# A two-layer hybrid mixer on one core: accumulators that share a PSUM tile are evacuated together

## The chip, the cores and the metric

The kernel runs on one core of a Trainium2 chip. The metric is the device time of one execution in microseconds: the median of three runs was 1438.51 us, the lowest 1437.9, the highest 1441.57.

## The reference, cut to what matters

Two layers (`DEPTH = 2`) work on 512 latent tokens ("x") and 256 context tokens ("c"), each 1024 channels wide. All arithmetic is float32. Each layer normalises both streams, projects them with one wide matrix `w_in`, runs three branches (a convolution of width 31, a chunked linear attention called GLA, and grouped-query attention), merges them with sigmoid gates and multiplies by `w_out`:

```python
hx = rms_norm(xs, norm_g) * (1 + scale_x[:, None]) + shift_x[:, None]
px = split_cols(hx @ w_in + b_in)
...
xs = xs + gate_x[:, None] * merge(px, ya_x, yb_x, yc_x)
if need_ctx:
    cs = cs + gate_c * merge(pc, ya_c, yb_c, yc_c)
```

`merge` ends with `@ w_out`. In the second layer the context stream is not written back, and attention queries are needed for the latent stream alone. The result is the latent stream.

## The kernel before

**Precision.** Every float32 operand of a large product is split into a rounded part and a remainder (`hi` and `lo`, `whi` and `wlo`), and a product is the sum of three: `hi*whi`, `lo*whi`, `hi*wlo`. A step of 256 input channels (two blocks of 128) for a tile of 128 tokens and 512 output columns is thus six matmuls (`tm_terms`, L566): four on `whi`, two on `wlo`.

**Weights.** `g_load` brings one unit of weights after the other into two `raw` buffers, `g_split` casts it into `whi` (ScalarE or VectorE) and subtracts for `wlo` (VectorE). There are three buffers of each.

**Two kinds of projections.** Most jobs compute channel-major results through single-bank PSUM tiles (`pg`, two of them; `pm`, two more). The jobs of class `Wide` (L650) compute token-major results: `QJob` (queries, with a bias added on the way out) and `OutJob` (the product with `w_out`). A `Wide` job holds one accumulator of 128 tokens by 512 columns for each token tile, and goes through the input channels in four rounds, one weight unit each; in a round every token tile gets its six matmuls in turn.

**Where the accumulators lie.** `banks` (L656) takes PSUM for them. The tag `p2` has two buffers of 1024 columns, and each of them holds the accumulators of two token tiles, side by side (`b[:, 0]` and `b[:, 1]`); `pg` and `pm` hold one each. `done` gives a `p2` buffer back when both of its accumulators have been read. The trace calls tiles of the tag `p2` just `p`. These jobs have pairs in `p2`:

- `QJob` of the first layer: six token tiles, two pairs in `p2` and two in `pg`
- `QJob` of the second layer: four token tiles, two pairs
- `OutJob` of the first layer for x: block 0 (columns 0 to 511) in two pairs, block 1 in `pg` and `pm`
- `OutJob` of the first layer for c: blocks 0 and 1, one pair each
- `OutJob` of the second layer for x: block 0 in two pairs, block 1 in `pg` and `pm`; the kernel ends with it

**Evacuation.** In the last round (`q == 3`), `mm` (L678) starts a thread `evac` for a token tile as soon as its matmuls have been written into the program. For a `QJob` it adds the bias on VectorE and writes to SBUF. For an `OutJob` (`out_ev`, L1868) VectorE multiplies the accumulator by the gate `gb` into `tg`, adds the result to the residual, and SyncE stores it. `gb` is a broadcast made on TensorE in the fourth round (`gate`, L1936) and copied out of PSUM by ScalarE or VectorE (`gev`).

**What sets the order.** The program is written at build time by a planner, `Weaver`: threads (Python generators) of different priorities announce the engine that they want next, and the planner, with its own table of costs, resumes whichever can run first. The order in which threads issue is the order of each engine's queue on the chip. `gemm` (L541) gives way to other threads after every three matmuls. Where a step may go to ScalarE or VectorE ("E"), the planner takes the one that it thinks is free first. The sequence of the large jobs is a list (`P["o0"]`, `P["o1"]`). The waits between the engines are set by the framework from the tiles that each instruction reads and writes; they are not written in the kernel.

**After the first layer's output jobs.** The c output jobs run on TensorE while the x stream is normalised for the second layer (`norm_g`, `norm_t`: squares on ScalarE and VectorE, a reciprocal root on GpSimd, scaling, transposes on TensorE, then the split into `hx`). The context follows the same way once its last output block is there, into `hc`. The second layer starts with `c2 m7 q1 q0`: two channel-major jobs that need `hx`, the `QJob`, and the key/value job, which needs `hc` too.

Of the kernel before, what the change touches and what calls it, by code (L numbers as in the profile page):

```python
# [105 lines left out]
class Weaver:  # L106
# [22 lines left out]
    def spawn(self, gen, prio):  # L129
        ready = self.cur.fin + self.LAT if self.cur else self.now  # L130
        th = _Thread(gen, prio, ready)
        i = 0
        while i < len(self.threads) and self.threads[i].prio <= prio:
            i += 1
        self.threads.insert(i, th)
        self._resume(th, keep=True)
# [35 lines left out]
    def need(self, *tags):  # L172
        def ok():
            return all(sum(a <= self.now for a in self.avail[t]) >= n for t, n in tags)
        if not ok():
            yield ok
        for t, n in tags:
            for _ in range(n):
                self.avail[t].remove(min(self.avail[t]))
# [11 lines left out]
    def free(self, tag, n=1, low=False):  # L191
        if low:
            self.low -= n
        t = self.cur.fin + self.LAT
        self.avail[tag] += [t] * n
        self.marks.append(t)
# [5 lines left out]
    def wait(self, *evs):  # L202
        def ok():
            return all(e.t is not None and e.t <= self.now for e in evs)
        if not ok():
            yield ok
# [100 lines left out]
def hybrid_kernel(ctx: ExitStack, tc: tile.TileContext, x, c, ctx_in, c_ctx, norm_g, w_mod, b_mod,  # L307
# [75 lines left out]
    need, free, wait, fire, spawn = W.need, W.free, W.wait, W.fire, W.spawn  # L383
# [157 lines left out]
    def gemm(ps, terms, start=True, stop=True):  # L541
        n = len(terms)
        for i, (l, r) in enumerate(terms):
            if i % 3 == 0:
                yield "+P"
            PE.matmul(ps, lhsT=l, rhs=r, start=start and i == 0, stop=stop and i == n - 1)
# [19 lines left out]
    def tm_terms(w, h, cols, k0):  # L566
        wh, wl = w
        hh, hl = h
        t = []
        for k in range(wh.shape[1]):  # L570
            t += [(hh[:, k0 + k, cols], wh[:, k]), (hl[:, k0 + k, cols], wh[:, k])]
        for k in range(wh.shape[1]):
            t += [(hh[:, k0 + k, cols], wl[:, k])]
        return t
# [75 lines left out]
    class Wide:  # L650
# [5 lines left out]
        def banks(self, n, tags):  # L656

            took, left = [], n
            for t, k in tags:
                m = 2 if t == "p2" else 1  # L660
                while k and left > 0:
                    took.append((t, min(m, left)))
                    left -= m
                    k -= 1
            yield from need(*[(t, sum(x == t for x, _ in took)) for t in dict(took)])
            ps = []
            for t, m in took:
                hold = [m]
                b = {"p2": p2, "pg": pg, "pm": pm}[t]([m, 512])

                def done(hold=hold, t=t):
                    hold[0] -= 1
                    if hold[0] == 0:
                        free(t)
                ps += [(b[:, i], done) for i in range(m)]
            return ps

        def mm(self, tiles, ps, ready, evac, mid=None):  # L678
            for q, (i, u) in enumerate(zip(self.order, self.us)):
                yield from wait(u.ev)  # L680
                if mid is not None and q == 3:
                    yield from mid()
                for t, (h, rows) in enumerate(tiles):
                    yield from ready(i, t)
                    w, hl = u.w, h
                    yield from gemm(ps[t][0], tm_terms(w, hl, rows, 2 * i), start=q == 0, stop=q == 3)
                    if q == 3:
                        spawn(evac(t, *ps[t]), 1)
                free("whi")
                free("wlo")  # L690

# [1385 lines left out]
```

## Time and profile before

| | |
|---|---|
| median of three runs | 1438.51 us |
| the profiled execution | 1437.46 us |
| its span, first to last instruction | 1435.7 us |
| TensorE busy | 1384.6 us (96%) in 9076 matmuls |
| VectorE busy | 1059.7 us (74%) |
| ScalarE busy | 574.3 us (40%) |
| GpSimd busy | 233.8 us (16%) |
| granted TensorE clock | 1.000 |

The profiled execution lies 1.8 us over its span, and 1.05 us below the median. Every arithmetic instruction passes through one recording helper, so all rows carry its line, L302; they are told apart by their tiles. In a row of the timeline, the first number is the start in us, the second the time from the first start to the last end of a run of like instructions, then the engine, and in brackets the idle time of the engine before it and what ended that.

### The profile page before, as it was taken

How to read it: one execution, taken by the hardware profiler on the slowest of the kernel's cores; microseconds unless marked ns; L12 is line 12 of the kernel's file. 1: busy time of each engine (PE TensorE's matmuls, PEld its weight loads, DVE VectorE, ACT ScalarE, POOL GpSimd, SP SyncE). 2: the span in 40 equal slices, each digit the busy share in tenths (PEclk: the TensorE clock that was granted, in tenths of full speed). 3: DMA queues.
4: the chain of work that ended last, by engine and by line, in shares of the span. 5: the costliest groups of instructions: out<-in, count | busy, mean ns of one | idle time of the engine just before them, and what ended most of it. 6: DMA issues, size and time to landing. Idle time of an engine off the chain costs nothing.

```text
span 1435.7 us, 23778 instructions
## 1 busy us (share of the span) xinstructions
PE 1384.6 (96%) x9076; PEld 1187.9 (83%) x9076; DVE 1059.7 (74%) x1863; ACT 574.3 (40%) x1113; POOL 233.8 (16%) x325
## 2 busy tenths in 40 slices
PE   3999999999999999999999999999999999999998
PEld 2789888888998878788888778988888988778886
DVE  4437966689946999963676485877679999997664
ACT  4514455554215324442322163345554155344320
POOL 1004212231000041310031020512221000231200
PEclk9999999999999999999999999999999999999999
DMA  9931233123342335554654365432224344345752
GB/s 271 289 110 51 72 103 90 47 58 89 92 128 75 103 114 165 158 159 154 213 192 146 122 197 181 125 108 79 61 59 115 83 114 136 103 139 193 256 198 73
DMA packets 219157, 187.49 MB, mean 131 GB/s; under 512 B 15400, under 2 KB 181922, under 8 KB 219044
## 3 DMA queue, kind: packets, MB, share of 16 engines
q1 hardware_dynamic: 218748, 185.87, 42.8%
q8 instruction: 71, 1.16, 0.3%
q14 instruction: 42, 0.34, 0.1%
q10 hardware_dynamic: 296, 0.11, 0.0%
HBM read 151.86 MB, written 34.08 MB: 130 GB/s over the span
## 4 chain that ended last, share of the span: by engine, by line
PE 50%; DVE 5%; POOL 1%; issue 1%; ACT 1%; DMA 0%; SPq 0%; DVEq 0%; POOLq 0%
PE pg L302 36%; PE p L302 9%; PE pm L302 4%; DVE r L302 3%; POOL sm L302 1%; DVE tg L302 1%; DVE wlo L302 1%; DVE t L302 0%; DMA r<-oad 0%; DVE zt L302 0%; POOL r L302 0%; ACT r L302 0%; ACT tg L302 0%; DVE sm L302 0%; ACT whi L302 0%
## 5 line engine op out<-in xcount | busy, mean ns | idle before, releaser
L302 PE MATMUL pg<-hx,whi 128*128 128x512 f32 x1504 | 385.8, 397 | 0.3 <-DVE r L302 0.3
L302 PEld LDWEIGHTS pg<-hx,whi 128*128 128x128 f32 x1504 | 272.3, 188 | 54.8 <-issue 2.8
L302 DVE SCALAR_TENSOR_TENSOR r<-r,tp,r 128x768 f32<-128x768 f32 (+29 forms) x240 | 201.2, 883 | 0.2
L302 PE MATMUL pg<-hx,wlo 128*128 128x512 f32 x752 | 196.4, 394 | 0.0
L302 ACT CAST whi<-raw 128x512 fp32r<-128x512 f32 (+1 forms) x195 | 115.0, 619 | 191.6 <-PE pg L302 113.4
L302 DVE TENSOR_TENSOR wlo<-raw,whi 128x1024 fp32r<-128x1024 f32 (+1 forms) x140 | 173.7, 1241 | 17.1 <-ACT whi L302 16.2
L302 PEld LDWEIGHTS pg<-hx,wlo 128*128 128x128 f32 x752 | 138.3, 188 | 27.7 <-issue 0.4
L302 ACT ACTIVATE tg<-pg,hv 128x256 f32<-128x256 f32 (+1 forms) x116 | 71.8, 619 | 186.7 <-PE pg L302 163.5
L302 DVE TENSOR_TENSOR r<-r,r 128x512 f32<-128x512 f32 (+8 forms) x208 | 119.1, 599 | 24.7 <-DMA r<-ogd 9.0
L302 PE MATMUL pg<-r,whi 128*128 128x512 f32 (+1 forms) x576 | 124.8, 358 | 0.3 <-DVE tg L302 0.2
L302 POOL TENSOR_SCALAR r<-r,sm 128x768 f32<-128x768 f32 (+1 forms) x80 | 78.6, 985 | 273.1 <-DVE sm L302 222.5
L302 PEld LDWEIGHTS pg<-r,whi 128*128 128x128 f32 x576 | 96.1, 188 | 17.6 <-DVE tg L302 0.7
L302 PE MATMUL pg<-hc,whi 128*128 128x256 f32 x768 | 105.0, 285 | 0.0
L302 DVE TENSOR_TENSOR r<-p,r 128x384 fp32r<-128x384 f32 (+2 forms) x152 | 77.8, 544 | 33.8 <-ACT r L302 27.6
L302 PEld LDWEIGHTS pg<-hc,whi 128*128 128x128 f32 x768 | 98.4, 190 | 3.3 <-issue 0.4
L302 ACT ACTIVATE r<-p,sm 128x768 f32<-128x768 f32 (+1 forms) x80 | 65.4, 818 | 83.8 <-DVE sm L302 81.1
L302 PE MATMUL p<-r,r 64*64 64x128 f32 (+3 forms) x800 | 84.8, 299 | 4.1 <-DVE r L302 2.9
L302 POOL TENSOR_TENSOR r<-r,r 128x512 f32<-128x512 f32 (+1 forms) x33 | 48.3, 1469 | 224.3 <-DVE r L302 219.4
L302 DVE CAST whi<-raw 128x512 fp32r<-128x512 f32 (+1 forms) x85 | 35.5, 422 | 64.1 <-PE p L302 26.8
L302 PE MATMUL pg<-whi,hx 128*128 128x272 f32 (+2 forms) x480 | 82.4, 309 | 0.0
L302 PE MATMUL pm<-r,r 128*128 128x256 f32 (+3 forms) x832 | 81.4, 279 | 0.2
L302 PEld LDWEIGHTS p<-r,r 64*64 64x64 f32 (+2 forms) x800 | 65.7, 163 | 17.5 <-issue 7.4
(171 smaller groups left out, 2091.6 us busy)
## 6 DMA issues: line engine op xcount, KB each, us to landing
raw<-in_w_in SPq DMA_DIRECT2D x116, 512.0 KB
r<-in_w_mod SPq DMA_DIRECT2D x64, 192.0 KB
thd<-tg SPq DMA_DIRECT2D x48, 256.0 KB
raw<-in_w_out SPq DMA_DIRECT2D x24, 512.0 KB
r<-thd SPq DMA_DIRECT2D x24, 384.0 KB
r<-in_w_mod SPq DMA_DIRECT2D x16, 384.0 KB
sgd<-tg SPq DMA_DIRECT2D x24, 256.0 KB
r<-thd SPq DMA_DIRECT2D x24, 256.0 KB
```

What stands on the lines that cost most here:

```text
L302: return real(*a, **k)
```

## The change

The list that `banks` returns says for each accumulator, beside its PSUM slice and its `done`, whether it is the last one of its PSUM tile. In the last round `mm` no longer starts an accumulator's `evac` thread right behind its own matmuls: it keeps the token tiles in `full`, and starts their threads, in order, once the matmuls of the last accumulator of the same PSUM tile have been written. For tiles in `pg` and `pm`, which hold one accumulator, nothing changes. The list of jobs and the parameters of the planner stay as they are.

```diff
@@ banks
-                ps += [(b[:, i], done) for i in range(m)]
+                ps += [(b[:, i], done, i == m - 1) for i in range(m)]
@@ mm
+                full = []
                 for t, (h, rows) in enumerate(tiles):
                     yield from ready(i, t)
                     w, hl = u.w, h
                     yield from gemm(ps[t][0], tm_terms(w, hl, rows, 2 * i), start=q == 0, stop=q == 3)
-                    if q == 3:
-                        spawn(evac(t, *ps[t]), 1)
+                    full.append(t)
+                    if q == 3 and ps[t][2]:
+                        for t in full:
+                            spawn(evac(t, *ps[t][:2]), 1)
+                        full = []
```

## Rows read from the trace of the kernel before

**Rows 1.** The page: busy time of each engine, with share of span and instructions.
```profile
PE 1384.6 (96%) x9076; PEld 1187.9 (83%) x9076; DVE 1059.7 (74%) x1863; ACT 574.3 (40%) x1113; POOL 233.8 (16%) x325
```

**Rows 2.** The page: the chain that ended last, share of span by engine.
```profile
PE 50%; DVE 5%; POOL 1%; issue 1%; ACT 1%; DMA 0%; SPq 0%; DVEq 0%; POOLq 0%
```

**Rows 3.** Stretches: start:end, length; busy us of PE, PEld, DVE, ACT, POOL; clock.
```profile
520.00:590.00 70.00, 67.20 (x640) 57.64 (x640) 66.67 (x95) 26.00 (x47) 16.54 (x29) 1.00 0.56 158
...
896.00:960.00 64.00, 64.00 (x483) 56.23 (x482) 50.63 (x103) 23.95 (x52) 19.42 (x36) 1.00 0.42 120
...
1090.00:1230.00 140.00, 139.72 (x776) 122.11 (x775) 137.21 (x225) 55.90 (x96) 1.73 (x3) 1.00 0.43 118
1230.00:1300.00 70.00, 65.05 (x610) 51.85 (x609) 64.04 (x119) 28.45 (x47) 20.89 (x33) 1.00 0.39 129
```

**Rows 4.** What PE waited for: us in total, times, longest.
```profile
PE p L302 <- DVE tg L302: 6.9, 6, 2.7
PE p L302 <- DVE r L302: 5.4, 10, 1.0
```

**Rows 5.** Timeline of PE: two gemms of six, first round of block 0.
```profile
780.38 1.07 PE L302 MATMUL p<-whi,hx 128*128 128x512 f32 x4
...
781.74 1.07 PE L302 MATMUL p<-whi,hx 128*128 128x512 f32 x4
```

**Rows 6.** Timeline of PE: last round of that job, the first pair's second gemm.
```profile
798.96 0.86 PE L302 MATMUL p<-whi,hx 128*128 128x512 f32 x3
800.67 0.50 PE L302 MATMUL p<-whi,hx 128*128 128x512 f32 x1 [0.85 <-DVE tg L302]
...
801.47 1.07 PE L302 MATMUL p<-whi,hx 128*128 128x512 f32 x4
```

**Rows 7.** Timeline of DVE beside it.
```profile
799.93 0.69 DVE L302 TENSOR_TENSOR tg<-p,r 128x512 f32<-128x512 f32 x1 [1.60 <-PE p L302]
```

**Rows 8.** Timeline of PE: first and last `QJob` stall, first `OutJob` stall at the end.
```profile
107.97 0.50 PE L302 MATMUL p<-whi,hx 128*128 128x512 f32 x1 [0.78 <-DVE r L302]
...
894.44 0.50 PE L302 MATMUL p<-whi,hx 128*128 128x512 f32 x1 [0.79 <-DVE r L302]
...
1403.66 0.51 PE L302 MATMUL p<-whi,hx 128*128 128x512 f32 x1 [0.85 <-DVE tg L302]
```

**Rows 9.** Timeline of DVE: the first layer's `QJob`, its first pair.
```profile
105.19 1.29 DVE L302 TENSOR_TENSOR r<-p,r 128x512 f32<-128x512 f32 x2 [1.29 <-PE p L302]
```

**Rows 10.** Timeline of PE: block 0 of the c output job.
```profile
838.39 0.86 PE L302 MATMUL p<-whi,hc 128*128 128x512 f32 x3
841.98 0.49 PE L302 MATMUL p<-whi,hc 128*128 128x512 f32 x1 [2.73 <-DVE tg L302]
...
842.77 0.85 PE L302 MATMUL p<-whi,hc 128*128 128x512 f32 x3
843.47 1.03 PE L302 MATMUL pm<-cst,r 128*128 128x128 f32 x8
```

**Rows 11.** Timeline of ACT and DVE beside it.
```profile
840.63 0.57 ACT L302 COPY r<-pm 128x512 f32<-128x512 f32 x1
841.10 0.72 ACT L302 ACTIVATE r<-r,sm 128x512 f32<-128x512 f32 x1
...
841.23 0.69 DVE L302 TENSOR_TENSOR tg<-p,r 128x512 f32<-128x512 f32 x1 [0.74 <-ACT r L302]
841.84 0.48 DVE L302 TENSOR_SCALAR r<-r,sm 128x512 f32<-128x512 f32 x1
```

**Rows 12.** Timeline of DVE and PE: block 1 of the c output job and after.
```profile
858.41 1.21 DVE L302 TENSOR_TENSOR wlo<-raw,whi 128x1024 fp32r<-128x1024 f32 x1
859.54 0.68 DVE L302 TENSOR_TENSOR r<-r,tg 128x512 f32<-128x512 f32 x1
...
861.88 0.68 DVE L302 TENSOR_TENSOR r<-r,tg 128x512 f32<-128x512 f32 x1
...
870.25 0.84 PE L302 MATMUL pm<-cst,r 128*128 128x128 f32 x4
```

## The prediction

> **What bounds the kernel now.** I read the shares of the engines first: TensorE (PE) is busy 96% of the span, VectorE (DVE) 74% [rows 1]. The reader is to see that only about 51 us of TensorE's span are idle, so what can be won without removing work lies in those. The chain of waits says the same: of the stretch that it follows, TensorE holds ten times the share of VectorE [rows 2]. The view by stretches shows where the two come close: in 520 to 590 and 1230 to 1300 us TensorE has gaps while VectorE is nearly full, and in 1090 to 1230 both are full [rows 3]. Then I asked what TensorE waits for. One line is about this change alone: matmuls into `p` wait for VectorE writing `tg`, six times, 6.9 us in all, and `tg` is written from PSUM only in the evacuation of an `OutJob` [rows 4]. Two more such waits, on `r`, belong to the `QJob`s [rows 8].
>
> The timeline shows what they are. A gemm of six matmuls takes 1.36 us from its first start to the next gemm's (780.38 to 781.74) [rows 5]. In the last round the second gemm of a pair starts at 798.96, issues three, then stands for 0.85 us and goes on at 800.67 [rows 6]. In between VectorE reads the pair's *first* accumulator, from 799.93, after waiting for TensorE itself [rows 7]; it ends at 800.62, 0.05 us before TensorE resumes. So the two take turns on one PSUM tile though they touch different halves: the evacuation waits for the three matmuls written ahead of it, and the fourth waits for the evacuation. The place in the middle of the gemm follows from the code, which lets other threads in after three matmuls.
>
> **The change part by part.** No arithmetic instruction is added or removed. Ten first accumulators (the pairs listed above) are evacuated one gemm later, after the last matmul on their tile. Two pairs, the first of each `QJob`, have no stall now: in the first layer both evacuations already run back to back after the second gemm [rows 9]. Eight stalls go:
>
> Their idle times are 6.9 us (six) and 0.78 and 0.79 (two), together 8.5 us [rows 4, 8]. A stall costs more than its idle time, as the restarted pipeline is slower: from 798.96 to 801.47 are 2.51 us, 1.15 over the clean 1.36, of which 0.85 is idle [rows 5, 6]. With 0.30 for each of eight, TensorE loses 8.5 + 2.4 = 10.9 us. That is the most that the direct effect can give. Of the six, one is 2.73 us and two are 0.85 [rows 6, 8, 10], which leaves 2.5 us for three, 0.83 each. What arrives at the end, place by place:
>
> - *Second layer's x output, last job:* idle 0.85 [rows 8] and one of the 0.83, with 0.30 for each 2.3 us. Behind it are only matmuls and the end, so all of it counts: 2.3 (bounds 2.0, if a restart costs less, and 2.3).
> - *First layer's x output, block 0:* the same, 2.3 us, ahead of block 1, whose last evacuations start the norm of the second layer; the whole sequence moves up: 2.3 (bounds 1.0, if the norm's engines don't follow, and 2.3).
> - *c output, block 0:* the large one, 2.73 us idle. Here VectorE waits for a copy of the gate on ScalarE (840.63, 0.57), which sits behind the norm of x in ScalarE's queue [rows 10, 11]. The next thing in TensorE's queue but three is the transposes of the normalised x, at 843.47 [rows 10]. Their input is ready at 841.82 from ScalarE and 842.32 from VectorE, where the last piece stood behind the evacuation [rows 11]. With the stall gone TensorE runs into these transposes and waits there. Won is 843.47 less 842.3 or so: 1.0 us (bounds 0 and 2.73 + 0.30 = 3.0).
> - *c output, block 1:* idle 0.83, so 1.1. But here lies the price of the change: both evacuations now start after the gemm, and the context's norm waits for the second. Before, the adds were done at 860.22 and 862.56, the second behind a weight split [rows 12]. Four operations of 0.69 from about 858.4 (when the first multiply ended before; the gemm would end there now) end at 861.2 if the splits (1.21 each) come after them, at 863.6 if both come between. The transposes of the normalised context at 870.25 follow about 8 us after [rows 12]; they come 1.3 us earlier or 1.0 later, while TensorE would be there 1.1 us early. I take 0.5 (bounds -1.0 and 1.1).
> - *The two `QJob` stalls:* 0.78 + 0.30 and 0.79 + 0.30, 2.2 us in all, early in each layer. TensorE is full behind the second (64.00 of 64.00 us in 896 to 960), which hands the gain on, but GLA's stretches at 520 and 1230 hang on VectorE, busy 66.67 of 70 and 64.04 of 70 [rows 3], which may keep it. I take half, 1.1 (bounds 0 and 2.2).
>
> Sum: 2.3 + 2.3 + 1.0 + 0.5 + 1.1 = 7.2 us; bounds 2.0 and 10.9.
>
> What I cost at nothing: VectorE's burst of two multiplies and two adds in a row (2.8 us) is covered by its idle time before them (1.60 us ahead of the first) [rows 7] and by weight buffers split ahead. The `p2` buffer comes free with the last evacuation, at most 0.7 us later; no job that follows asks for it at once. The stores on SyncE's queue wait up to 1.4 us longer for their adds, and a weight load written behind one waits with it; two `raw` and three split buffers cover that. If such a load were needed at once it would cost these 1.4 us, in place of the gain of its block.
>
> The Trainium skill speaks against holding back: "Perfetto Trace Analysis", section "Matmuls", says that independent matmul groups should rotate through different PSUM banks so that the evacuation of one overlaps the next group's matmuls. By it the old order is the right one, the two accumulators need no turns, and the change would only delay evacuations. The trace shows the turns all the same, 6.9 and 1.6 us of them [rows 4, 8]; the result by that rule is the third rival below.
>
> **The rivals.** *The plan comes out anew and takes the gain back.* The planner knows nothing of the stalls; for it the change only moves evacuations, and it may choose other engines and other places from there on. For the early jobs VectorE idles right after (1.29 us ahead of rows 9, for instance), so the plan should fall back into step. From the c output on it may not: the context's transposes get other places, and the whole second layer hangs on them. Against: TensorE's own work is the same whatever its order, and it has next to no gaps in 896 to 1230 [rows 3]. A loss of 3 to 11 us somewhere in the second layer leaves -4 to +4: about 1437.
>
> *Slower: GLA of the second layer.* VectorE is busy 137.21 of 140 us in 1090 to 1230 and 64.04 of 70 after; TensorE stands for 70 - 65.05 = 5 us in the latter [rows 3]. If the new order puts a few convolution taps or weight splits ahead of the GLA steps for which TensorE waits, each puts 0.7 to 1.2 us in its way. Doubling the gap of 5 us takes most of the gain; tripling it adds 10, and over 11.5 added us the kernel is slower by more than 4.3. Some ten such operations would be needed; tripled and a little more gives 1438.5 - 7.2 + 13 = 1444.3. For it speaks VectorE's load, against it that the list of jobs stands.
>
> *The waits stay, or were not about the tile.* If TensorE's waits have another cause, evacuation is only later: c block 1 loses up to 1.0 us, and the time is 1438.5 to 1439.5. Against it: the resumption 0.05 us after the evacuation's end [rows 6, 7].
>
> *All arrives.* The direct bound of 10.9 us, or a plan that happens to be better: 1427.6 or a little less.
>
> **How the numbers follow.** The sum is made against the profiled execution (1437.46 us, span 1435.7), which lies 1.05 us under the median; I subtract it from the median, 1438.51 - 7.2 = 1431.3. Chances: the forecast (1428.5 to 1434) 0.56; all or more 0.09; the plan takes the gain back 0.19; slower through GLA 0.12; waits stay 0.04. The range takes in the bound below with a little luck, 1426.5, and above the case of the gain taken back, 1438.5. This kernel's measurement can tell about 0.3%, 4.3 us, from no change: faster is below 1434.2, slower above 1442.8. Faster: 0.56 + 0.09 + 0.02 of the third case = 0.67. Slower: 0.11 of the 0.12. The rest, 0.22, is the same.
>
> **What would show it.** In the changed profile TensorE's waits into `p` on `tg` should be gone or under 1 us; the second gemm of each last round should take 1.36 us; VectorE should read both halves of a pair back to back; TensorE should stand for 1 to 2 us ahead of the transposes of x in the c output. The last job should be about 2.3 us shorter from its first matmul on `p` to the end. The prediction is wrong if these waits go and TensorE's idle time turns up in the second layer instead, above all between 1090 and 1300 us, or if the order of TensorE's queue differs already in the first layer's attention.

## The result and the profile after

The changed kernel took 1430.62 us (median of four runs, 1428.96 to 1431.54), the kernel before 1439.18 us beside it (four runs, 1437.9 to 1441.57). The ratio is 0.9935, with a 95% interval of 0.9924 to 0.9947: faster by some 9 us, against a forecast of 7.2.

The page of the changed kernel: busy time of the engines.

```profile
PE 1382.8 (97%) x9076; PEld 1187.9 (83%) x9076; DVE 1058.7 (74%) x1866; ACT 572.6 (40%) x1110; POOL 233.2 (16%) x325
```

The work is the same [rows 1]: 9076 matmuls, and three operations have gone from ScalarE to VectorE. The difference lies in what TensorE waits for (us in total, times, longest):

```profile
PE pm L302 <- ACT t L302: 3.1, 4, 1.1
...
PE p L302 <- DVE r L302: 4.2, 9, 1.0
```

The row of six waits into `p` on `tg` [rows 4] is gone, and the waits on `r` are one fewer and 1.2 us shorter. In their place TensorE waits longer for ScalarE's copy of the transposes of x out of `pm` into `t`; in the kernel before this row was

```profile
PE pm L302 <- ACT t L302: 1.4, 2, 1.0
```

The same places on TensorE's timeline: the first `QJob`, the first layer's x output and the last job.

```profile
105.77 1.07 PE L302 MATMUL p<-whi,hx 128*128 128x512 f32 x4
...
107.13 1.07 PE L302 MATMUL pg<-whi,hx 128*128 128x512 f32 x4
...
797.35 1.08 PE L302 MATMUL p<-whi,hx 128*128 128x512 f32 x4
...
798.72 1.07 PE L302 MATMUL p<-whi,hx 128*128 128x512 f32 x4
...
1395.76 1.08 PE L302 MATMUL p<-whi,hx 128*128 128x512 f32 x4
...
1397.13 1.07 PE L302 MATMUL p<-whi,hx 128*128 128x512 f32 x4
```

Each pair's second gemm now goes through without a break: 797.35 to 798.72 is 1.37 us, as in a round without evacuation [rows 5], where 2.51 us stood before [rows 6]. VectorE reads both halves one after the other, and adds both (the x output, then block 1 of the c output):

```profile
798.99 1.29 DVE L302 TENSOR_TENSOR tg<-p,r 128x512 f32<-128x512 f32 x2 [2.28 <-PE p L302]
800.20 1.28 DVE L302 TENSOR_TENSOR r<-r,tg 128x512 f32<-128x512 f32 x2
...
854.67 1.28 DVE L302 TENSOR_TENSOR tg<-p,r 128x512 f32<-128x512 f32 x2
855.87 1.28 DVE L302 TENSOR_TENSOR r<-r,tg 128x512 f32<-128x512 f32 x2
```

The stretches that [rows 3] show, on the changed kernel (start:end, length; busy us of PE, PEld, DVE, ACT, POOL; clock):

```profile
520.00:590.00 70.00, 68.01 (x655) 58.21 (x655) 67.03 (x95) 26.47 (x48) 15.88 (x25) 1.00 0.58 166
896.00:960.00 64.00, 64.00 (x462) 55.20 (x461) 51.71 (x104) 27.89 (x59) 20.41 (x33) 1.00 0.40 116
1090.00:1230.00 140.00, 139.92 (x810) 122.19 (x808) 137.05 (x225) 52.75 (x89) 0.41 (x2) 1.00 0.42 120
1230.00:1300.00 70.00, 65.09 (x569) 51.77 (x570) 63.17 (x115) 32.00 (x52) 23.57 (x37) 1.00 0.40 135
```

VectorE is as full as it was, and TensorE stands no longer in the last stretch (4.91 us against 4.95): no new gap in the second layer.

To see where the time came from, I cut the span at fixed matmuls that every version has, such as the first of a job, and took the differences of their starts in the timeline. Lengths in us (profiled executions):

| Stretch between two matmuls | before | after | difference |
|---|---|---|---|
| span's start to the first `QJob` | 77.79 | 77.21 | -0.58 |
| A: first `QJob`, to the next job | 33.73 | 32.64 | -1.09 |
| B: to the first layer's x output | 668.86 | 668.92 | +0.06 |
| C: its block 0 | 24.88 | 22.67 | -2.21 |
| D: its block 1 and the c output, to the second layer's first matmul on `hx` | 54.09 | 52.82 | -1.27 |
| E: to the second layer's key/value job, second `QJob` within | 35.90 | 34.56 | -1.34 |
| F: to the last job | 488.10 | 488.33 | +0.23 |
| G: its block 0 | 24.93 | 22.70 | -2.23 |
| H: its block 1, to the last add | 23.64 | 23.59 | -0.05 |

The sum is -8.48, and the span went from 1435.7 to 1427.2. The first row is not the change's: the order there is the same, and it is the first transfers that land a little earlier or later from run to run. The change itself gives 7.9 us in these two profiles. Short stretches repeat to 0.02 us from run to run, the long ones do not: with the changed kernel run a second time D was 53.40 and F 488.46, and of another kernel run twice B was 669.55 and 668.86. Differences under 0.7 us in B, D and F prove nothing by themselves.

By the names of their tiles, TensorE's matmuls stand in the same order in both profiles up to 836 us and again from 875 us on (times of the changed kernel). Only between the two, in the c output and the second `QJob`, did transposes and matmuls change places. The planner fell back into step, so no better order of TensorE's in the rest of the second layer brought the gain.

### The profile page after: what moved, and what is told of

It reads as the page before. It is cut to its first block, busy times and chain, and to the rows that moved or that the text cites. A ratio compares the mean times of both kernels' runs of the same rounds, so it can differ in the third digit from the quotient of the medians.

```text
span 1427.2 us, 23779 instructions
## 1 busy us (share of the span) xinstructions
PE 1382.8 (97%) x9076; PEld 1187.9 (83%) x9076; DVE 1058.7 (74%) x1866; ACT 572.6 (40%) x1110; POOL 233.2 (16%) x325
## 4 chain that ended last, share of the span: by engine, by line
PE 49%; DVE 5%; POOL 1%; issue 1%; ACT 1%; DMA 0%; SPq 0%; DVEq 0%; POOLq 0%; ACTq 0%
PE pg L302 37%; PE p L302 8%; PE pm L302 4%; DVE r L302 3%; POOL sm L302 1%; DVE wlo L302 1%; DVE tg L302 1%; DVE t L302 0%; ACT r L302 0%; DMA r<-oad 0%; DVE zt L302 0%; POOL r L302 0%; ACT tg L302 0%; ACT whi L302 0%; ACT t L302 0%
```

## The experiments

My theory: evacuation and matmuls take turns on a whole PSUM tile; holding the first evacuation back removes these turns, and each removed wait counts up to the next thing TensorE waits for. The rivals: the waits belong to the bank or the place and not to the tile; or the gain comes from a luckier plan and the waits are incidental. The letters A to H are those of the table.

### Held back in the last job alone

```diff
-                    if q == 3 and ps[t][2]:
+                    if q == 3 and (ps[t][2] or not (isinstance(self, OutJob) and self.L.last)):
```

> The pairs are held together only in the x output of the second layer (the last job); everything before it is issued as in the kernel before. Theory (the two halves of a pair take turns on one PSUM tile): the two waits of 0.8 us in block 0 of the last job go, each with some 0.3 us of slower restart, so the time falls by 2.2 us (2.0 to 2.3), and the six stalls of the earlier jobs stay (about 6 us idle). Rival (the waits have another cause, holding back only makes evacuation later): the waits stay and the time is the same or up to 0.7 us longer.

Measured: 1437.24 us (11 runs) against 1439.69 (21 runs), ratio 0.9983 (0.9974 to 0.9992), 2.4 us faster. G and the rest behind it agree with 2.2: with nothing behind it but matmuls, a job keeps the whole of two waits and their restarts. The waits that are left:

```profile
PE p L302 <- DVE tg L302: 5.2, 4, 2.7
```

Two of six waits and 1.7 of 6.9 us are gone [rows 4].

### Waits removed without a later evacuation

The evacuations stay where they were in the kernel before, but the second gemm of a pair is issued in one go in the last round, so that the first accumulator's read is written into the program behind it (here `ps[t][2]` is the accumulator's place in its PSUM tile, 0 or 1):

```diff
-    def gemm(ps, terms, start=True, stop=True):
+    def gemm(ps, terms, start=True, stop=True, step=3):
...
-            if i % 3 == 0:
+            if i % step == 0:
...
-                    yield from gemm(ps[t][0], tm_terms(w, hl, rows, 2 * i), start=q == 0, stop=q == 3)
-                    if q == 3:
-                        spawn(evac(t, *ps[t]), 1)
+                    yield from gemm(ps[t][0], tm_terms(w, hl, rows, 2 * i), start=q == 0, stop=q == 3,
+                                    step=6 if q == 3 and ps[t][2] else 3)
+                    if q == 3:
+                        spawn(evac(t, *ps[t][:2]), 1)
```

> Evacuations are started right behind their own accumulator as before, but the second accumulator of a pair issues its last six matmuls without giving way after three. Theory that the wait works on the whole PSUM tile: the first evacuation, though it is early in VectorE's queue, begins only after the sixth matmul of the second accumulator; all eight stalls go and the time falls like that of the changed kernel, by 7 to 9 us. Rival, that only the place in the middle of the gemm matters and the tile does not: the first evacuation begins about 0.25 us after its own last matmul, beside the second gemm; stalls go as well, with VectorE 1.4 us earlier than in the changed kernel.

Measured: 1433.89 us (5 runs), ratio 0.9961 (0.9949 to 0.9974), 5.6 us faster, less than expected. All eight waits are gone. TensorE and VectorE at the first pair of the x output:

```profile
799.16 1.08 PE L302 MATMUL p<-whi,hx 128*128 128x512 f32 x4
800.08 0.62 PE L302 MATMUL p<-wlo,hx 128*128 128x512 f32 x2
...
800.80 0.69 DVE L302 TENSOR_TENSOR tg<-p,r 128x512 f32<-128x512 f32 x1 [2.28 <-PE p L302]
```

This is the plainest view of the turn-taking. The gemm of the first accumulator had ended before 799.4 (the second's starts at 799.16); VectorE, idle for 2.28 us, reads it at 800.80, 0.10 us after the last matmul on the *other* half (800.08 + 0.62 = 800.70). VectorE waits for the tile's last written matmul, not for its own accumulator's.

A, C and G came out as in the changed kernel (32.64, 22.67, 22.69). What was lost lies in E, 38.33 us against 34.56, where the transposes of the normalised context kept their old place ahead of the `QJob` (TensorE; then a stretch with its clock, the eighth number after the length):

```profile
867.74 0.33 PE L302 MATMUL pm<-cst,r 128*128 128x128 f32 x1 [1.48 <-ACT r L302]
868.35 0.76 PE L302 MATMUL pm<-cst,r 128*128 128x128 f32 x3 [0.28 <-ACT r L302]
868.76 2.06 PE L302 MATMUL p<-whi,hx 128*128 128x512 f32 x4
...
869.00:872.00 3.00, 3.00 (x10) 2.31 (x10) 2.16 (x4) 1.44 (x4) 0.00 (x0) 0.51 0.96 342
```

TensorE arrives early, waits 1.76 us for the norm, and then runs at about half clock (0.51, the 1.2 GHz level) for 3 us: four matmuls take 2.06 us instead of 1.08. D was shorter first (51.97 us against 54.09 before); over D and E together six at once took 90.30 us, the kernel before 89.99 and the changed kernel 87.38.

### Held back in all but the c output, and in the c output alone

```diff
-                    if q == 3 and ps[t][2]:
+                    if q == 3 and (ps[t][2] or not (not (isinstance(self, OutJob) and self.s == "c"))):
```

> Held together in all jobs but the two c output blocks. Theory of the ledger (two query stalls 1.1 each, two x outputs 2.2 each, the c blocks 1.2): 5.5 to 7 us faster than before, the stalls of 2.7 and 0.85 us in the c blocks are still there. Rival, that the redrawn order of the second layer, which comes from the c blocks, brought a good part of the 8.5 us: under 5 us faster.

Measured: 1433.3 us (5 runs), ratio 0.9959 (0.9946 to 0.9971), 5.9 us faster.

```diff
-                    if q == 3 and ps[t][2]:
+                    if q == 3 and (ps[t][2] or not (isinstance(self, OutJob) and self.s == "c")):
```

> Held together only in the two c output blocks; the second layer's order is redrawn as in the changed kernel. Theory: both c stalls go (4.1 us with restart), but the transposes of the normalised x limit the gain at the start of the second layer to 1.2 us, and 1 to 2 us arrive at the end. Rival (the c stalls count in full): 4 us. Rival (the redrawn order costs or brings more than the stalls): outside 0 to 2.5 us.

Measured: 1437.46 us (11 runs), ratio 0.9984 (0.9975 to 0.9993), 2.3 us faster. The two halves add up: 5.9 + 2.3 = 8.2 us, and the whole change, run once more beside other runs below, gave 0.9943 (0.993 to 0.9955), 8.2 us. Each of these gains is known to about 1.5 us. So within that each place keeps its own gain, and no luck of the plan is needed. What is left of the waits in the one and the other:

```profile
PE p L302 <- DVE tg L302: 3.6, 2, 2.7
```

```profile
PE p L302 <- DVE tg L302: 3.3, 4, 0.9
```

In the profile of "c alone", D is 54.12 us, no shorter than before. TensorE has traded the wait of 2.73 us for three at the transposes of x:

```profile
844.65 0.66 PE L302 MATMUL pm<-cst,r 128*128 128x128 f32 x4 [1.06 <-ACT t L302]
...
852.79 0.66 PE L302 MATMUL pm<-cst,r 128*128 128x128 f32 x4 [1.07 <-ACT t L302]
...
854.12 0.66 PE L302 MATMUL pm<-cst,r 128*128 128x128 f32 x4 [0.67 <-ACT t L302]
```

That the runs gain 2.3 us all the same probably has a second source. The wait of 2.73 us stands in five profiles: before, "last job alone", "all but c", and two of the versions further down ("Blocks' PSUM exchanged" and "A longer read"). Behind it the clock fell to 0.50 in "last job alone", "all but c" and "Blocks' PSUM exchanged", and stayed at 1.00 in the other two. In "last job alone" and "all but c" D is 55.69 us, 1.6 more than before with the same instructions. From "last job alone":

```profile
843.18 0.49 PE L302 MATMUL p<-whi,hc 128*128 128x512 f32 x1 [2.73 <-DVE tg L302]
...
844.95 1.91 PE L302 MATMUL pm<-cst,r 128*128 128x128 f32 x8
...
845.00:847.00 2.00, 2.00 (x10) 1.99 (x9) 1.75 (x3) 0.88 (x2) 0.00 (x0) 0.50 0.33 127
```

Here the clock fell to half behind the wait, and eight transposes took 1.91 us; in the profile of before they took 1.03 [rows 10], at full clock:

```profile
844.00:846.00 2.00, 2.00 (x15) 1.70 (x14) 1.97 (x4) 1.90 (x4) 0.00 (x0) 1.00 0.27 100
```

So the long wait has a price that shows in some executions only, in three of these five. The mean granted clocks on record point the same way, though they don't say where in the span it fell: a loss of 1.6 us in 1436 lowers the mean by about 0.001 (an estimate), and the kernel before had a mean of 1.000 in 8 of the 59 executions beside the experiments, the changed kernel in 7 of 9, "c alone" in 5 of 11. That this is what "c alone" gained is not shown: its executions at 1.000 were no shorter than its others.

### The gate of the c output earlier

The kernel before, with the gate's broadcast in the second round for c, so that its copy on ScalarE comes ahead of the norm of x:

```diff
-                if mid is not None and q == 3:
+                if mid is not None and q == (1 if self.s == "c" else 3):
```

> The kernel before, with one thing moved: in the two c output jobs the gate broadcast is made ahead of the second round instead of the fourth, so that its copy on ScalarE is not stuck behind the norm of x when the first c accumulator is evacuated. Theory: the wait of 2.73 us in c block 0 is 0.85 of turn-taking and 1.9 of that late copy; it becomes about 0.8, the transposes of x bound what arrives at the second layer's start to 0 to 1.2 us, and where the granted clock fell after the long wait another 1.6 us come back: 0.5 to 3 us faster, not more. Rival (the long wait counts in full on the path, whatever the transposes do): 1.9 us at the start of the second layer in executions whose clock stays at 1.0. The other seven waits stay.

Measured: 1441.34 us (11 runs), ratio 1.001 (1.0001 to 1.0019): slower by 1.7 us, where I had expected a gain. The long wait shrank as meant (`p` on `tg` is down to 3.7 us in five waits, 0.9 the longest), but the planner now put the transposes of x ahead of it, and TensorE ran into them:

```profile
842.45 0.33 PE L302 MATMUL pm<-cst,r 128*128 128x128 f32 x1 [2.55 <-ACT r L302]
...
843.67 0.77 PE L302 MATMUL pm<-cst,r 128*128 128x128 f32 x5 [0.90 <-ACT r L302]
```

The cause named in the prediction for this wait was right (a copy of the gate queued behind the norm [rows 11]), and removing the cause still won nothing: 2.73 us became 2.55 + 0.90, as TensorE now waited for the scaled x itself, whose last piece ScalarE ended at 843.62. Of the longer stretches E shows the loss most clearly, 36.66 us against 35.90: two more waits, 0.29 and 0.28 us, at the transposes of the context. The rest of the 1.7 us is open. The clock may have a part in it: this profile has 1.00 throughout, but the mean was 1.000 in three of the eleven executions only (1439.63 to 1440.96 us; the others 1440.93 to 1442.71).

### Later still

The changed kernel, with a pair's evacuations held until the last `p2` pair of the job is done:

```diff
-                    if q == 3 and ps[t][2]:
+                    if q == 3 and (ps[t][2] and not any(p[2] is False for p in ps[t + 1:])):
```

> Held back further than in the change: a job's accumulators in p are evacuated only when the last pair is finished (the first pair 2.7 us later than in the changed kernel; the c blocks, with one pair, as in it). Theory, that later evacuation costs nothing where VectorE is idle and nobody waits: no waits on p, and the time of the changed kernel, 1430.6 within 2 us, if the plan of the early jobs stays. Rival (promptness counts): slower than the changed kernel by 2.7 us or more.

Measured: 1433.42 us (4 runs), ratio 0.9961 (0.9947 to 0.9974), by the medians 2.8 us slower than the change. That is the number of the rival, but not its place: in the jobs themselves the lateness cost nothing (A 32.64, C 22.68, G 22.72, as in the changed kernel). The loss is in F, 491.07 us against 488.33. Here the planner did draw the second layer's order anew: TensorE's queue is that of the changed kernel up to 900 us and then differs in some fifty places. In the new order there is a long wait in the stretch from 1230 to 1300 us:

```profile
1255.52 0.63 PE L302 MATMUL pm<-cst,t 128*128 128x128 f32 x4 [2.89 <-DVE t L302]
...
1256.00:1260.00 4.00, 4.00 (x11) 2.50 (x10) 4.00 (x6) 0.00 (x0) 0.00 (x0) 0.57 0.60 150
```

In the changed kernel the longest wait for VectorE's `t` was 1.2 us there. Behind the wait of 2.89 us the clock stood at 0.57 for 4 us, a loss of 1.7 us against full clock. So in this one profile the larger part of the 2.7 us in F is the clock's, and the new order's only by way of the wait. This is the rival "the plan comes out anew", but its size in other executions is not shown (the four took 1432.81 to 1437.71 us).

### Blocks' PSUM exchanged

The kernel before, with block 0 of an x output in `pg` and `pm` and block 1 in `p2` (the gate's pool exchanged too):

```diff
-            ps = yield from self.banks(n, (("p2", 2),) if blk == 0 or n < 4 else (("pg", 2), ("pm", 2)))
+            ps = yield from self.banks(n, (("p2", 2),) if blk == 1 or n < 4 else (("pg", 2), ("pm", 2)))
```

> The kernel before, with the PSUM of the two blocks of the x output jobs exchanged: block 0 takes the four single tiles (pg, pm), block 1 the two pairs (p). Theory that the shared tile makes the wait: in the last rounds of both x output jobs block 0 has no wait on tg, and block 1 has two of about 0.8 us instead; total within 2 us of the kernel before. Rival (the wait belongs to the first block of a job or to the evacuation as such): the waits stay in block 0 or are in both.

Measured: 1439.66 us (10 runs), ratio 1.0 (0.9991 to 1.0009). The four waits left block 0 and appeared in block 1 with the same lengths:

```profile
824.35 0.51 PE L302 MATMUL p<-whi,hx 128*128 128x512 f32 x1 [0.85 <-DVE tg L302]
828.15 0.50 PE L302 MATMUL p<-whi,hx 128*128 128x512 f32 x1 [0.78 <-DVE tg L302]
...
1428.81 0.49 PE L302 MATMUL p<-whi,hx 128*128 128x512 f32 x1 [0.85 <-DVE tg L302]
1432.62 0.50 PE L302 MATMUL p<-whi,hx 128*128 128x512 f32 x1 [0.78 <-DVE tg L302]
```

The wait goes where the two-bank tile goes. It belongs neither to a block nor to the gate, which is fetched in both. How an accumulator is read that has a tile to itself shows in block 1 of the changed kernel's last job (TensorE, then VectorE):

```profile
1417.96 0.63 PE L302 MATMUL pg<-wlo,hx 128*128 128x512 f32 x2
1418.43 1.08 PE L302 MATMUL pg<-whi,hx 128*128 128x512 f32 x4
...
1418.70 0.69 DVE L302 TENSOR_TENSOR tg<-pg,r 128x512 f32<-128x512 f32 x1 [11.78 <-PE pg L302]
```

The read begins 0.11 us after its own last matmul (1418.59), beside the next gemm in the other `pg`, which doesn't break off. The same two banks of `p2` taken as two tiles were not run.

### A longer read

The kernel before, where the first accumulators of the last job's two pairs are multiplied four times (the same product each time):

```diff
-            V.tensor_mul(o, ps, job.gb)
+            for _ in range(4 if S.last and blk == 0 and i % 2 == 0 else 1):
+                V.tensor_mul(o, ps, job.gb)
```

> The kernel before, and in block 0 of the last job the multiply that reads the first accumulator of each of the two pairs is issued four times instead of once (same result; 3 x 0.6 to 0.7 us more on VectorE each time). Theory (TensorE stands for as long as the first half is being read): the two waits grow from 0.85 and 0.78 to 2.7 to 3.0 us and the time by 3.6 to 4.4 us; if the granted clock then falls to 0.5 for some 3 us, as it did in one profile after the wait of 2.73 us in the c output, up to 1.6 us more for each. Rival (the wait ends with something else than the read): it stays near 0.8 us and the time grows by under 1 us.

Measured: 1441.65 us (12 runs), ratio 1.0019 (1.0011 to 1.0028), 3.0 us slower by the medians, below the 3.6 that I had expected at the least. The first pair did as the theory says:

```profile
1403.83 2.87 DVE L302 TENSOR_TENSOR tg<-p,r 128x512 f32<-128x512 f32 x4 [1.61 <-PE p L302]
...
1406.75 0.51 PE L302 MATMUL p<-whi,hx 128*128 128x512 f32 x1 [3.03 <-DVE tg L302]
...
1409.00:1412.00 3.00, 3.00 (x11) 2.36 (x10) 0.70 (x2) 0.38 (x1) 0.00 (x0) 0.68 0.46 175
...
1412.09 3.46 DVE L302 TENSOR_TENSOR tg<-p,r 128x512 f32<-128x512 f32 x5 [2.39 <-PE p L302]
```

Three more reads of 0.73 us made TensorE's wait 3.03 instead of 0.85 us [rows 8], 2.18 longer, and it goes on 0.05 us after VectorE's end (1406.70). The second pair has no wait at all: with VectorE taken for longer, the planner wrote its reads (1412.09) behind both gemms, which is the change by accident. G grew by 2.70 us, from 24.93 to 27.63: 2.19 for the first pair, 1.60 for a clock that fell behind the wait of 3.03 us (the next two gemms take 2.55 and 1.77 us instead of 1.36 each), less 1.08 for the second pair's wait.

### The changed kernel, and its next wait removed

In the changed kernel TensorE waits for the norm of x in the c output. In the second layer the norm's reciprocal root is a chain of small operations on GpSimd, in the first a shorter one on VectorE. This version takes the VectorE form in both:

```diff
-            if S.l == 0:
+            if True:
```

> The changed kernel, and in the norm of the second layer the sums and the Newton steps of the reciprocal root go to VectorE, as the first layer has it; GpSimd keeps the power alone. Theory that the norm's chain on GpSimd, some 8.5 us, now sets what the c blocks can give: normalised x is ready 2 us or more earlier, TensorE's 2.7 us of waiting for transposes in the c blocks shrink to under 1, and the time falls 1 to 3 us below the changed kernel. Rival: VectorE, nearly full there, takes the place of GpSimd: same time within 1 us, or slower through the redrawn second layer.

Measured: 1429.0 us (4 runs), ratio 0.9923 (0.991 to 0.9937). This lies close to the changed kernel's own time, so both were run again on one chip, with the kernel before beside them:

> The changed kernel once more, beside the next one on the same chip: 7.5 to 9.5 us faster than before.

> The changed kernel with the root of the second layer's norm on VectorE once more, beside the changed kernel: 1 to 2 us faster than that, if the gain is real; the same, if the 1.6 us were the chip or the day.

Measured: the changed kernel 1430.97 us (5 runs, 1429.38 to 1431.76), ratio 0.9943 (0.993 to 0.9955); with the root on VectorE 1428.77 us (5 runs, 1427.38 to 1429.34), ratio 0.9927 (0.9915 to 0.9939). No run of the one reaches into those of the other; the version is 2.2 us faster than the change and beats both kernels. The intervals against before overlap all the same, so the size is rough. The change alone has this chain on GpSimd (first and last row of 14), and TensorE's wait behind it:

```profile
827.62 1.25 POOL L302 TENSOR_TENSOR sm<-sm 128x1 f32<-128x1 f32 x2 [54.06 <-DVE t L302]
...
835.93 0.20 POOL L302 TENSOR_TENSOR sm<-sm,sm 128x2 f32<-128x2 f32 x1
...
839.82 0.66 PE L302 MATMUL pm<-cst,r 128*128 128x128 f32 x4 [1.06 <-ACT t L302]
...
848.01 0.66 PE L302 MATMUL pm<-cst,r 128*128 128x128 f32 x4 [0.67 <-ACT t L302]
```

With the root on VectorE two GpSimd rows are left, and the first of the two waits, at the third block of transposes, is gone in both of its profiles (the other one has 0.49 us at the eighth); the 0.67 us now stand at the broadcast behind them:

```profile
829.15 1.65 POOL L302 TENSOR_TENSOR sm<-sm,mhalf 128x2 f32<-128x2 f32 x1 [55.62 <-DVE sm L302]
832.95 0.81 POOL L302 TENSOR_TENSOR sm<-sm,mhalf 128x2 f32<-128x2 f32 x1 [2.15 <-DVE sm L302]
...
848.76 1.12 PE L302 MATMUL pm<-yg,cst 128*128 128x512 f32 x2 [0.67 <-ACT t L302]
```

D is 51.06 and 51.79 us in its two profiles, 52.82 and 53.40 in the two of the change. The waits of this kind in D were 1.7 and 2.1 us there, not the 2.7 of the expectation.

## Why the prediction was right, point by point

**The mechanism.** Right, and shown in three ways. With the turns removed by another means (six matmuls in one go) all eight waits go; with the tile moved they move; with a longer read the one wait that is left there grows by the length of the read. The Trainium skill, "PSUM — Partial Sum Buffer", section "Summary: rules for kernel authors", advises to read PSUM during matmuls from a different bank and to guard it by bank. By the size that the page gives a bank (section "Specifications (TRN2)"), 512 float32 columns, the two accumulators lie in different banks here. The trace of six at once shows the read waiting all the same, from before 799.4 to 800.80, for the last matmul in the other bank. So another bank was not enough while both were one tile.

**The third rival, that the waits stay**, which rested on the rule of rotating banks, fell with that.

**x outputs, 2.3 each.** C gave 2.21, G 2.23, H was unchanged. The restart that I put at 0.30 measures about 0.3: two waits of 0.85 and 0.78 us are 1.63, and (2.21 - 1.63) / 2 = 0.29.

**c output, 1.0 + 0.5.** D gave 1.27 in the one profile of the change and 0.69 in the other, and of E's 1.34 some 0.26 is left beside the `QJob`'s 1.08: 1.0 to 1.5 us together, about as forecast. That it fits is partly luck, for it did not come about as I had it block by block. I had TensorE standing ahead of the *first* transposes of x, for the normalised x. They lost only about 0.4 us (1.46 us instead of 1.03), and the waits came 3 and 11 us later, 1.06 and 0.67 us, at transposes further on in the same norm. What these waited for was a free `pm` buffer: ScalarE, working through the scalings of x, came late to the copy that empties it:

```profile
839.01 1.44 ACT L302 ACTIVATE t<-pm,shx,scx 128x512 f32<-128x512 f32 x2
```

The first of these two copies ended at about 839.73, and TensorE went on at 839.82. And the price that I set against block 1, a later norm of the context, was not paid: in the changed kernel the planner put the context's transposes behind two and a half gemms of the `QJob`, where before they stood ahead of it at 870.25 [rows 12]:

```profile
865.14 1.07 PE L302 MATMUL p<-whi,hx 128*128 128x512 f32 x4
...
868.55 0.60 PE L302 MATMUL pm<-cst,r 128*128 128x128 f32 x4
```

The price is real where they stay: with six at once E was 38.33 us, where 35.90 less the `QJob`'s 1.08 are 34.82. That is 3.5 us in E, of which D had given 2.1 before; over both, with the `QJob`'s 1.08 taken out, the c output lost 1.4 us where it was to gain 1.5. The fall of the clock alone cost some 1.6 us there, and for that I had no term. The profile of before also hid a part of the term: executions in which the clock falls behind the wait of 2.73 us paid 1.6 us more, and "c alone" gained 2.3 us by the ratio, though its own profile shows next to none of it.

**The two `QJob` stalls, 1.1.** This is the term that was mis-sized. I took half of 2.2, since VectorE's stretches in GLA might keep the rest. B and F came out 0.06 and 0.23 us longer, which is within their scatter: of 1.09 + 1.08 = 2.17 us about 1.9 or more arrived. The stall's own 1.08 in E is seen by itself in "all but c", where E is 34.82 against 35.90. An earlier start reaches VectorE too, and a full engine behind it just starts earlier; I had mistaken "nearly full" for "tied to a fixed time".

**The plan taking the gain back, and slower through GLA.** Neither happened in the change: F is 0.23 us longer, TensorE's order is the old one from 875 us on, and 1230 to 1300 has the gap that it had. "Held until the last pair" shows that both were fair rivals: a new order, and by it a longer wait (2.89 us) in that very stretch, cost 2.7 us in one profile. Nothing that I ran came near the 13 us of the second.

**The total.** 7.2 us forecast, 7.9 in the profiles with the 0.58 of the start left out, 9.4 by the ratio (7.6 to 10.9 by its interval), 8.2 when run again. The 0.7 between forecast and profiles is the `QJob` term's. Both profiles have a clock of 1.000, so what the runs show beyond 7.9 may be the price of the long wait, which the sum does not have; that is not shown.

## What to carry to other kernels

When the matmul engine waits in the middle of a group for a reader, look at whether the reader touches another part of the same tile: here waits worked on the allocated tile, so two accumulators in one tile were one accumulator for the purpose of evacuation. They should then be read when both are done or be given tiles of their own. Price such a wait by its idle time plus the restart, and then walk on to the next thing that the engine needs, for a removed wait is worth no more than the lead that this lets through. Of a long wait, look at the granted clock behind it in several executions before saying what it costs.

## What the runs showed of the hardware

- A wait of TensorE cost about 0.3 us beyond its idle time (stretches A, C, E and G).
- After a wait of 2.73 us the granted clock was 0.50 over the next stretch in the profile of "last job alone" and 1.00 in the profile of before, with the same instructions on TensorE ahead of it (of five profiles with this wait, three show a fall; after 2.55 us in "the gate earlier" it stayed at 1.00); after 1.76 us in two waits it was 0.51, after 2.89 us 0.57 over 4 us, after 3.03 us 0.68 over the stretch from 1409 to 1412. After 2.73 and after 3.03 us the fall cost 1.6 us. What decides between the two I can't tell from these runs.
